# High parts of a seven-product pair in one tile of the large pool: a fp32 decoder block on one core of Trainium2

## The chip, the cores and the metric

One core of a Trainium2 chip runs the whole program. The metric is the device time of one execution in microseconds (us), taken as the median of several runs.

## The reference

One layer of a decoder on 256 tokens with a width of 2048, all in fp32. What matters here are its matrix products with large weights:

```python
u = rmsnorm(h, g_mix[i]);  proj = u @ w_in[i]
out_a = attn @ w_attn_br[i]          # sliding-window attention
out_s = y @ w_ssd_br[i]              # Mamba-2 SSD branch
merged = sigmoid(g_a) * out_a + sigmoid(g_s) * out_s
h = h + merged @ w_o[i]
f = rmsnorm(h, g_ffn[i])
h = h + (silu(f @ w_gate[i]) * (f @ w_up[i])) @ w_down[i]
h = h + sigmoid(rmsnorm(h, g_ple[i]) @ w_ple_gate[i]) * (p[i] @ w_ple_proj[i])
return rmsnorm(h, g_final)
```

## The kernel before

A fp32 weight is split into a high part (a cast to fp32r on ScalarE, ACT) and a low part (weight minus high part, on VectorE, DVE). A product is then three matmuls on TensorE (PE): high times high, high times low, low times high. PE does little else than these.

`wide_block` (L281) multiplies the 256 tokens (two blocks of 128) with two column blocks of 512 and runs over the contraction in k-pairs of 2 x 128. It serves the last gate columns of `w_in` (GSO, two calls), `w_ssd_br` (two), `w_o` (two), eleven blocks of gate and up (`hidden`, called hidden 0 to 10 here), and `w_down`, which is cut into thirds that run after hidden 3, 7 and 10 (two calls each). For each k-pair there are two kinds of work:

- A *plain* pair: for each of the two column blocks a load of 512 KB into a buffer `wr` (SP's queue, L298), the cast `wh` of 1024 columns (L309), the subtraction `wl` (L311), and 24 matmuls (L249) in all.
- A *seven-product* pair (two block products in seven instead of eight, for the pairs in `forms`; 40 in the program): two loads, four additions of 512 columns on DVE into `tr` (L329), then casts (L337) and subtractions (L338) of three items: the whole first load (1024 columns), one half of the second load (512 columns), and `tr` (2048 columns, into `th` and `tl`), and 21 matmuls.

Buffers come from rotating pools: `wraw` has 4 (for `wr`), `whi` 4 (for `wh`), `wlo` 3 (for `wl`), each of 1024 columns (4 KB per partition), and `big` 17 of 8 KB, for `tr`, `th`, `tl`, the token matrices and more. A tile waits until the buffer that it gets is no longer read.

`pump` calls queued small work between the k-pairs: transposes of results on PE (L150) with their copies to SBUF (L137, L132 on ACT, L139, L133 on DVE), the token sums that the seven-product pairs multiply with (`fsc`, `fm`, `hforms`, `aforms`, L256 to L278), and sums of squares (`junk`, L1037).

The order of the instructions on each engine is not written by hand: a scheduler places them when the program is built, by when it takes operands and buffers to be ready. Each engine then runs its own list in that order. So a change of buffers moves instructions.

Of the kernel before, what the change touches and what calls it, by code (L numbers as in the profile page):

```python
# [12 lines left out]
F32R = mybir.dt.float32r  # L13
# [5 lines left out]
P = 128  # L19
# [4 lines left out]
NB = 512  # L24
# [37 lines left out]
def block_kernel(ctx: ExitStack, tc: tile.TileContext, x, x_t, p_t, positions, vecs, rows, g_final,  # L62
# [7 lines left out]
    whi_p = ctx.enter_context(tc.tile_pool(name="whi", bufs=4))  # L70
    wlo_p = ctx.enter_context(tc.tile_pool(name="wlo", bufs=3))
# [5 lines left out]
    def big(shape, dtype=F32, name="big"):  # L77
        return big_p.tile(shape, dtype, name=name, tag="big")
# [18 lines left out]
    def pump(n):  # L97
        for _ in range(n):
            for q in (side, heads):
                if q:  # L100
                    q.popleft()()
# [179 lines left out]
    def wide_block(halves, lhs, nk, forms, pumps=1):  # L281

        psum.reverse()
        np_, ns = nk // 2, len(forms)  # L290
        c11, c12, c21, c22 = sums = [
            Sums(acc_tile, 2 * (np_ - ns) + (ns if i < 3 else 0)) for i in range(4)]
        shared, done = None, 0
        parts = [None] * 4

        def load(q, kp, dst):
            w, col0 = halves[q]
            nc.sync.dma_start(out=dst, in_=w[2 * kp * P:2 * (kp + 1) * P, col0:col0 + NB].rearrange(  # L298
                "(k p) n -> p k n", p=P))

        for kp in range(np_):
            ev, od = lhs(2 * kp), lhs(2 * kp + 1)
            tok = [[[x[:, t * P:(t + 1) * P] for x in k] for k in (ev, od)] for t in range(NT)]
            if kp not in forms:
                for q in range(2):
                    wr = wraw_p.tile([P, 2, NB], F32, name="wr", tag="wr")
                    load(q, kp, wr)
                    wh = whi_p.tile([P, 2, NB], F32R, name="wh", tag="wh")
                    nc.scalar.copy(out=wh, in_=wr)  # L309
                    wl = wlo_p.tile([P, 2, NB], F32R, name="wl", tag="wl")  # L310
                    nc.vector.tensor_tensor(out=wl, in0=wr, in1=wh.bitcast(F32), op=ALU.subtract)  # L311
                    for k in range(2):
                        for t in range(NT):
                            sums[2 * t + q].add(tok[t][k], (wh[:, k], wl[:, k]))
                    pump(pumps)
                continue
            if shared is None:
                shared = [Sums(aux_tile, ns) for _ in range(4)]
            q1, q5, q6, q7 = shared
            a, g2, f3, s3 = [[forms[kp][:, i, 0], forms[kp][:, i, 1]] for i in range(4)]  # L320
            raw = [wraw_p.tile([P, 2, NB], F32, name="wr", tag="wr") for _ in range(2)]
            for q in range(2):
                load(q, kp, raw[q])
            tr = big([P, 4, NB], F32, name="tr")
            for o, x, y in ((tr[:, 0], raw[0][:, 0], raw[1][:, 0]),
                            (tr[:, 1], raw[1][:, 0], raw[1][:, 1]),
                            (tr[:, 2], tr[:, 1], raw[0][:, 0]),
                            (tr[:, 3], tr[:, 2], raw[0][:, 1])):
                nc.vector.tensor_tensor(out=o, in0=x, in1=y, op=ALU.add)  # L329
            split = []  # L330
            for x, xh, xl in (
                    (raw[0], whi_p.tile([P, 2, NB], F32R, name="wh", tag="wh"),
                     wlo_p.tile([P, 2, NB], F32R, name="wl", tag="wl")),
                    (raw[1][:, 1:2], whi_p.tile([P, 2, NB], F32R, name="wh", tag="wh")[:, 1:2],
                     wlo_p.tile([P, 2, NB], F32R, name="wl", tag="wl")[:, 1:2]),
                    (tr, big([P, 4, NB], F32R, name="th"), big([P, 4, NB], F32R, name="tl"))):
                nc.scalar.copy(out=xh, in_=x)  # L337
                nc.vector.tensor_tensor(out=xl, in0=x, in1=xh.bitcast(F32), op=ALU.subtract)  # L338
                split.extend((xh[:, i], xl[:, i]) for i in range(x.shape[1]))
            b11, b21, b22, t1, t3, t2, t4 = split  # L340
            q1.add(tok[0][0], b11)
            c11.add(tok[0][1], b21)
            c12.add(f3, b22)
            q6.add(g2, t2)
            q7.add(s3, t3)
            q5.add(a, t1)
            c21.add(tok[1][1], t4)
            pump(2 * pumps)
            done += 1
            if done == ns:  # L350
                mid = big([P, 4, NB], F32, name="mid")
                parts = [mid[:, i] for i in range(4)]
                nc.scalar.copy(out=parts[0], in_=q1.tile)
                for o, x, y, op in ((3, 0, q6, ALU.subtract), (2, 3, q7, ALU.add),
                                    (1, 3, q5, ALU.add), (3, 2, q5, ALU.add)):
                    nc.vector.tensor_tensor(out=parts[o], in0=parts[x], in1=y.tile, op=op)
        return [x.tile for x in sums], parts
# [649 lines left out]
    for jj in range(2):  # L1007
        sums, parts = wide_block(column_pair(w_in, GSO, jj), lhs_u, KD, uforms)
        for i in range(4):
            settle(i, sums, parts)  # L1010
            nc.scalar.activation(out=parts[i], in_=parts[i], func=AF.Sigmoid,
                                 scale=r1[:, i // 2:i // 2 + 1])
        gates.append(parts)
    mforms = form_tiles((5,), "mforms")
    for jj in range(2):
        sums, parts = wide_block(column_pair(w_ssd_br, 0, jj), lambda k: stat(yT, k), KD, yforms)
        for i in range(4):
            t, c = i // 2, cols(2 * jj + i % 2)
            settle(i, sums, parts)
            nc.vector.scalar_tensor_tensor(out=parts[i], in0=parts[i], scalar=r2[:, t:t + 1],  # L1020
                                           in1=gates[jj][i], op0=ALU.mult, op1=ALU.mult)
            nc.vector.tensor_tensor(out=merged[t][:, c], in0=merged[t][:, c], in1=parts[i],
                                    op=ALU.add)
        for q in range(2):
            queue_flip(merged, mergedT, 2 * jj + q, None, mforms)
# [19 lines left out]
    for jj in range(2):  # L1045
        add_to_h(jj, *wide_block(column_pair(w_o, 0, jj), lambda k: stat(mergedT, k), KD, mforms))
        for q in range(2):
            queue_flip(h, hT, 2 * jj + q, V_GFFN, hforms)
            side.append(lambda j=2 * jj + q: square_sum(j, ssq3))
# [135 lines left out]
    for c in range(KD // 4):  # L1185
# [3 lines left out]
        wh = whi_p.tile([P, 2, NB], F32R, name="wh", tag="wh")  # L1189
        nc.scalar.copy(out=wh, in_=wr)  # L1190
        wl = wlo_p.tile([P, 2, NB], F32R, name="wl", tag="wl")
# [73 lines left out]
```

## Time and profile before

| | |
|---|---|
| median of 3 runs | 1595.82 us (1594.87 to 1597.53) |
| the profiled execution | 1594.49 us, its span 1592.8 us |
| busy: PE, DVE, ACT | 99%, 75%, 53% of the span |
| chain of work that ended last | PE 92%, DVE 2%, DMA 2%, ACT 2%, issue 1% |
| mean granted clock of PE | 0.998 |

How to read it: the busy share of PE is modelled and says only that it hardly rests. The places where it does rest, and what ends each rest, are in the waits and in the timeline. A row of the timeline gives the start, the time, engine, line and operation, output and inputs, and in brackets the idle time before it with what ended it. Loads are issued on SP; the view of DMA gives the time from issue to landing.

### The profile page before, as it was taken

How to read it: one execution, taken by the hardware profiler on the slowest of the kernel's cores; microseconds unless marked ns; L12 is line 12 of the kernel's file. 1: busy time of each engine (PE TensorE's matmuls, PEld its weight loads, DVE VectorE, ACT ScalarE, POOL GpSimd, SP SyncE). 2: the span in 40 equal slices, each digit the busy share in tenths (PEclk: the TensorE clock that was granted, in tenths of full speed). 3: DMA queues.
4: the chain of work that ended last, by engine and by line, in shares of the span. 5: the costliest groups of instructions: out<-in, count | busy, mean ns of one | idle time of the engine just before them, and what ended most of it. 6: DMA issues, size and time to landing. Idle time of an engine off the chain costs nothing.

```text
span 1592.8 us, 19985 instructions
## 1 busy us (share of the span) xinstructions
PE 1574.0 (99%) x7298; PEld 1300.5 (82%) x7298; DVE 1201.3 (75%) x1507; ACT 844.2 (53%) x1073; POOL 132.1 (8%) x136
## 2 busy tenths in 40 slices
PE   9999999999999999999999999999999999999997
PEld 7988888888888888788788888788888878888886
DVE  8776766666666768788888788887878788788874
ACT  6654665555644554445655554455545444556653
POOL 1014224143210000000000000000000000000000
PEclk9999999999999999999999999999999999999999
DMA  8666435555646666655566655566665566655672
GB/s 270 177 198 185 136 105 158 158 161 157 178 157 183 210 199 213 209 195 189 173 199 195 198 188 197 185 210 193 193 196 177 194 203 199 220 189 185 200 228 87
DMA packets 152562, 296.63 MB, mean 186 GB/s; under 512 B 9536, under 2 KB 9664, under 8 KB 152080
## 3 DMA queue, kind: packets, MB, share of 16 engines
q1 hardware_dynamic: 151168, 290.76, 58.3%
q0 software_dynamic: 576, 3.47, 0.7%
q8 instruction: 57, 0.93, 0.2%
q10 hardware_dynamic: 720, 1.14, 0.2%
q14 instruction: 41, 0.34, 0.1%
HBM read 293.23 MB, written 2.10 MB: 185 GB/s over the span
## 4 chain that ended last, share of the span: by engine, by line
PE 92%; DVE 2%; DMA 2%; ACT 2%; issue 1%; POOL 0%; POOLq 0%; DVEq 0%; SPq 0%; ACTq 0%
PE aux L249 29%; PE acc L249 27%; PE acc L204 9%; PE acc L206 9%; PE acc L205 9%; PE aux L150 1%; DMA wr<-in_w_in_dram 1%; PE aux L754 1%; DMA wr<-in_w_gate_dram 1%; ACT th L337 1%; PE acc L150 1%; DVE tl L338 1%; PE aux L935 1%; PE aux L693 0%; ACT sc L899 0%
## 5 line engine op out<-in xcount | busy, mean ns | idle before, releaser
L309 ACT CAST wh<-wr 128x1024 fp32r<-128x1024 f32 x280 | 293.6, 1053 | 269.4 <-PE acc L249 97.2
L311 DVE TENSOR_TENSOR wl<-wr,wh 128x1024 fp32r<-128x1024 f32 x280 | 337.3, 1221 | 88.2 <-issue 35.8
L195 DVE TENSOR_TENSOR wl<-wr,wh 128x1024 fp32r<-128x1024 f32 (+1 forms) x172 | 227.6, 1330 | 119.6 <-PE acc L205 87.4
L193 ACT CAST wh<-wr 128x1024 fp32r<-128x1024 f32 (+1 forms) x172 | 173.7, 1013 | 167.9 <-PE acc L206 125.6
L249 PE MATMUL aux<-wh,flipT 128*128 128x512 f32 x736 | 237.8, 392 | 0.0
L249 PE MATMUL acc<-wh,flipT 128*128 128x512 f32 x640 | 208.4, 393 | 0.0
L204 PE MATMUL acc<-wh,uT 128*128 128x512 f32 (+1 forms) x512 | 200.3, 391 | 0.7 <-ACT cb L481 0.7
L206 PE MATMUL acc<-wh,uT 128*128 128x512 f32 (+1 forms) x512 | 194.2, 379 | 0.0
L205 PE MATMUL acc<-wl,uT 128*128 128x512 f32 (+1 forms) x512 | 193.9, 379 | 0.0
L249 PEld LDWEIGHTS aux<-wh,flipT 128*128 128x128 f32 x736 | 138.1, 188 | 28.3
L249 PE MATMUL aux<-wl,flipT 128*128 128x512 f32 x368 | 143.8, 391 | 0.6 <-DVE wl L311 0.6
L337 ACT CAST wh<-wr 128x1024 fp32r<-128x1024 f32 x80 | 66.8, 837 | 140.2 <-PE aux L249 62.4
L249 PEld LDWEIGHTS acc<-wh,flipT 128*128 128x128 f32 x640 | 120.2, 188 | 24.6 <-ACT wh L337 0.2
L249 PE MATMUL acc<-wl,flipT 128*128 128x512 f32 x320 | 124.6, 389 | 0.0
L338 DVE TENSOR_TENSOR tl<-tr,th 128x2048 fp32r<-128x2048 f32 x40 | 91.7, 2292 | 26.2 <-ACT th L337 26.1
L204 PEld LDWEIGHTS acc<-wh,uT 128*128 128x128 f32 x512 | 96.3, 188 | 18.1 <-issue 1.4
L205 PEld LDWEIGHTS acc<-wl,uT 128*128 128x128 f32 x512 | 96.4, 188 | 17.6 <-issue 1.0
L206 PEld LDWEIGHTS acc<-wh,uT 128*128 128x128 f32 x512 | 96.2, 188 | 17.8
L337 ACT CAST th<-tr 128x2048 fp32r<-128x2048 f32 x40 | 76.5, 1911 | 51.7 <-DVE tr L329 51.7
L249 PE MATMUL aux<-wh,actT 128*128 128x512 f32 x292 | 95.3, 393 | 0.0
L249 PE MATMUL acc<-wh,actT 128*128 128x512 f32 x292 | 93.6, 390 | 0.0
L338 DVE TENSOR_TENSOR wl<-wr,wh 128x1024 fp32r<-128x1024 f32 x80 | 76.2, 954 | 7.8 <-PE aux L249 4.0
(476 smaller groups left out, 2741.4 us busy)
## 6 DMA issues: line engine op xcount, KB each, us to landing
wr<-in_w_in_dram SPq DMA_DIRECT2D x144, 512.0 KB, 3.7
wr<-in_w_gate_dram SPq DMA_DIRECT2D x88, 512.0 KB, 3.7
wr<-in_w_up_dram SPq DMA_DIRECT2D x88, 512.0 KB, 4.1
wr<-in_w_down_dram SPq DMA_DIRECT2D x88, 512.0 KB, 4.4
wr<-in_w_ssd_br_dram SPq DMA_DIRECT2D x32, 512.0 KB, 4.3
wr<-in_w_o_dram SPq DMA_DIRECT2D x32, 512.0 KB, 4.0
wr<-in_w_ple_gate_dram SPq DMA_DIRECT2D x32, 512.0 KB, 4.9
wr<-in_w_in_dram SPq DMA_DIRECT2D x32, 256.0 KB, 3.9
```

Of the source, the lines that this page charges most:

```text
L150: nc.tensor.transpose(out=ps[:, j, t * P:(t + 1) * P], in_=src[t][:, c:c + P], identity=ident)
L193: nc.scalar.copy(out=wh, in_=wr)
L195: nc.vector.tensor_tensor(out=wl, in0=wr, in1=wh.bitcast(F32), op=ALU.subtract)
L204: nc.tensor.matmul(o, hi[:, ts], wh[:, kk, cs], start=(k == 0), stop=False)
L205: nc.tensor.matmul(o, hi[:, ts], wl[:, kk, cs], start=False, stop=False)
L206: nc.tensor.matmul(o, lo[:, ts], wh[:, kk, cs], start=False, stop=(k == nk - 1))
L249: nc.tensor.matmul(self.tile, a, b, start=self.first, stop=self.left == 0)
L309: nc.scalar.copy(out=wh, in_=wr)
L311: nc.vector.tensor_tensor(out=wl, in0=wr, in1=wh.bitcast(F32), op=ALU.subtract)
L337: nc.scalar.copy(out=xh, in_=x)
L338: nc.vector.tensor_tensor(out=xl, in0=x, in1=xh.bitcast(F32), op=ALU.subtract)
L754: nc.tensor.matmul(ps[:, es], m[:, t, e, :], xd[:, t, 0, es], start=True, stop=True)
```

## The change

The pair takes one more buffer of the `big` pool, called `sh`, of four times 512 columns. It holds the high parts of the first load (2), of the half of the second (1), and the low part of that half (1). So a pair takes no buffer of `whi` (before: two) and one of `wlo` (before: two). The instructions are the same in number, kind and size.

```diff
             split = []
+
+            sh = big([P, 4, NB], F32R, name="sh")
             for x, xh, xl in (
-                    (raw[0], whi_p.tile([P, 2, NB], F32R, name="wh", tag="wh"),
-                     wlo_p.tile([P, 2, NB], F32R, name="wl", tag="wl")),
-                    (raw[1][:, 1:2], whi_p.tile([P, 2, NB], F32R, name="wh", tag="wh")[:, 1:2],
-                     wlo_p.tile([P, 2, NB], F32R, name="wl", tag="wl")[:, 1:2]),
+                    (raw[0], sh[:, 0:2], wlo_p.tile([P, 2, NB], F32R, name="wl", tag="wl")),
+                    (raw[1][:, 1:2], sh[:, 2:3], sh[:, 3:4]),
                     (tr, big([P, 4, NB], F32R, name="th"), big([P, 4, NB], F32R, name="tl"))):
                 nc.scalar.copy(out=xh, in_=x)
                 nc.vector.tensor_tensor(out=xl, in0=x, in1=xh.bitcast(F32), op=ALU.subtract)
```

The scheduler's order changes with it. On DVE, in the second block of `w_ssd_br`, with its seven-product pair, before:

```order
L329 TENSOR_TENSOR tr<-wr 128x512 x2
L311 TENSOR_TENSOR wl<-wr,wh 128x1024
L329 TENSOR_TENSOR tr<-tr,wr 128x512 x2
L338 TENSOR_TENSOR wl<-wr,wh 128x1024
L338 TENSOR_TENSOR tl<-tr,th 128x2048
L338 TENSOR_TENSOR wl<-wr,wh 128x512
L311 TENSOR_TENSOR wl<-wr,wh 128x1024 x3
```

and after:

```order
L329 TENSOR_TENSOR tr<-tr,wr 128x512
L338 TENSOR_TENSOR sh<-wr,sh 128x512
L329 TENSOR_TENSOR tr<-tr,wr 128x512
L338 TENSOR_TENSOR wl<-wr,sh 128x1024
L338 TENSOR_TENSOR tl<-tr,th 128x2048
L311 TENSOR_TENSOR wl<-wr,wh 128x1024 x3
```

The subtraction of 512 columns stood behind the one of 2048 and now stands ahead of it, and ahead of that of 1024.

On ACT, around the first seven-product pair of hidden 0 (`flipT`: copies of transposed h; `fsc`, `hforms`: token sums; `junk`: sums of squares), before:

```order
L309 CAST wh<-wr 128x1024 x6
L337 CAST wh<-wr 128x1024
L137 ACTIVATE flipT<-acc,vec 128x256 x2
L337 CAST wh<-wr 128x512
L137 ACTIVATE flipT<-acc,vec 128x256 x2
L256 ACTIVATE fsc<-acc,vec 128x256 x2
L309 CAST wh<-wr 128x1024
L1037 ACTIVATE junk,ssq_5704<-h 128x512
L277 CAST hforms<-fm 128x4x128
L1037 ACTIVATE junk,ssq_5704<-h 128x512 x2
L137 ACTIVATE flipT<-acc,vec 128x256
```

and after:

```order
L137 ACTIVATE flipT<-acc,vec 128x256
L256 ACTIVATE fsc<-acc,vec 128x256 x2
L1037 ACTIVATE junk,ssq_5692<-h 128x512 x2
L277 CAST hforms<-fm 128x4x128
L1037 ACTIVATE junk,ssq_5692<-h 128x512 x2
L137 ACTIVATE flipT<-acc,vec 128x256
L337 CAST sh<-wr 128x1024
L137 ACTIVATE flipT<-acc,vec 128x256
L337 CAST sh<-wr 128x512
L337 CAST th<-tr 128x2048
```

The pair's casts of 1024 and 512 columns (L337) stood ahead of `fsc`, and now stand behind it, `junk` and a further `flipT`.

On ACT, around the seven-product pairs of hidden 2 (hidden 6 reads alike), before:

```order
L337 CAST wh<-wr 128x1024
L132 CAST actT<-acc 128x512
L337 CAST wh<-wr 128x512
L132 CAST actT<-acc 128x512
L256 ACTIVATE fsc<-acc 128x256 x2
L309 CAST wh<-wr 128x1024
L277 CAST aforms<-fm 128x4x128
L309 CAST wh<-wr 128x1024
L337 CAST th<-tr 128x2048
```

and after:

```order
L132 CAST actT<-acc 128x512
L309 CAST wh<-wr 128x1024
L132 CAST actT<-acc 128x512
L309 CAST wh<-wr 128x1024
L256 ACTIVATE fsc<-acc 128x256 x2
L277 CAST aforms<-fm 128x4x128
L337 CAST sh<-wr 128x1024
L337 CAST sh<-wr 128x512
L337 CAST th<-tr 128x2048
L309 CAST wh<-wr 128x1024 x2
L337 CAST sh<-wr 128x1024
L337 CAST sh<-wr 128x512
```

The pair's casts moved behind two plain casts (L309), `fsc` and `aforms`.

## Rows read from the trace of the kernel before

**Rows 1.** The page's first part: busy time, share of the span, instructions.

```profile
PE 1574.0 (99%) x7298; PEld 1300.5 (82%) x7298; DVE 1201.3 (75%) x1507; ACT 844.2 (53%) x1073; POOL 132.1 (8%) x136
```

**Rows 2.** The chain that ended last: start, us, what.

```profile
583.92 27.20 PE aux L249 x120
```

**Rows 3.** Waits of PE: engine, line, waited for: total us, times, longest.

```profile
PE acc L249 <- DVE wl L338: 3.6, 3, 1.6
...
PE acc L249 <- DVE tl L338: 0.7, 1, 0.7
...
PE aux L249 <- DVE wl L311: 0.6, 1, 0.6
```

**Rows 4.** Lines 337, 338 and 329: ns min/median/max, first and last start, forms.

```profile
L337 ACT CAST wh<-wr x80: 610/838/1058, 507.4 to 1467.1; 128x1024 fp32r<-128x1024 f32 x40, 128x512 fp32r<-128x512 f32 x40
L337 ACT CAST th<-tr x40: 1895/1912/1919, 511.2 to 1468.2; 128x2048 fp32r<-128x2048 f32 x40
...
L338 DVE TENSOR_TENSOR wl<-wr,wh x80: 682/956/1226, 511.1 to 1472.4; 128x1024 fp32r<-128x1024 f32 x40, 128x512 fp32r<-128x512 f32 x40
...
L338 DVE TENSOR_TENSOR tl<-tr,th x40: 2286/2293/2294, 513.2 to 1470.2; 128x2048 fp32r<-128x2048 f32 x40
...
L329 DVE TENSOR_TENSOR tr<-wr x80: 680/686/694, 507.4 to 1464.4; 128x512 f32<-128x512 f32 x80
```

**Rows 5.** Timeline of PE, second GSO block and hidden 1: start, us, what.

```profile
532.86 0.50 PE L249 MATMUL aux<-wl,uforms 128*128 128x512 f32 x1 [0.15 <-DVE wl L338]
...
823.63 0.50 PE L249 MATMUL aux<-tl,hforms 128*128 128x512 f32 x1
```

**Rows 6.** Timeline of DVE and of PE, second block of w_ssd_br.

```profile
656.20 2.29 DVE L338 TENSOR_TENSOR tl<-tr,th 128x2048 fp32r<-128x2048 f32 x1 [0.85 <-ACT th L337]
...
659.15 0.50 PE L249 MATMUL acc<-wl,yforms 128*128 128x512 f32 x1 [1.65 <-DVE wl L338]
```

**Rows 7.** Timeline of ACT, PE and SP's queue, hidden 0.

```profile
765.78 1.05 ACT L337 CAST wh<-wr 128x1024 fp32r<-128x1024 f32 x1 [1.67 <-PE aux L249]
...
769.01 0.62 ACT L337 CAST wh<-wr 128x512 fp32r<-128x512 f32 x1 [0.78 <-PE aux L249]
...
775.62 0.46 ACT L137 ACTIVATE flipT<-acc,vec 128x256 fp32r<-128x256 f32 x1
...
775.05 0.48 PE L249 MATMUL acc<-wh,flipT 128*128 128x512 f32 x1
...
776.41 0.37 SPq L298 DMA_DIRECT2D wr<-in_w_gate_dram  x1
```

**Rows 8.** Hidden 2: ACT, SP's queue with the load's time to landing, PE.

```profile
859.71 0.66 ACT L256 ACTIVATE fsc<-acc 128x256 f32<-128x256 f32 x2 [0.76 <-DVE actT L133]
...
856.07 0.37 SPq L298 DMA_DIRECT2D wr<-in_w_up_dram  x1
...
wr<-in_w_up_dram SPq DMA_DIRECT2D x1, 512.0 KB, 4.1
...
863.50 0.39 PE L249 MATMUL acc<-wh,flipT 128*128 128x512 f32 x1
```

**Rows 9.** Hidden 4: SP's queue with the load's time to landing, PE.

```profile
1030.23 0.37 SPq L298 DMA_DIRECT2D wr<-in_w_up_dram  x1
...
wr<-in_w_up_dram SPq DMA_DIRECT2D x1, 512.0 KB, 5.5
...
1039.75 0.50 PE L249 MATMUL acc<-tl,hforms 128*128 128x512 f32 x1
```

**Rows 10.** Second w_o block: SP's queue, the first load's time to landing, PE.

```profile
740.35 7.46 SPq L298 DMA_DIRECT2D wr<-in_w_o_dram  x3
...
wr<-in_w_o_dram SPq DMA_DIRECT2D x1, 512.0 KB, 5.2
...
749.49 0.39 PE L249 MATMUL aux<-tl,mforms 128*128 128x512 f32 x1
```

**Rows 11.** Stretches: us, busy us by engine, granted clock, DMA share, GB/s.

```profile
657.00:659.20 2.20, 0.55 (x4) 0.13 (x2) 2.20 (x3) 2.20 (x4) 0.00 (x0) 1.00 0.58 194
```

## The prediction

> **What bounds the kernel now.** I read the page first, then the waits of TensorE (PE), the rows by line, and PE's timeline at every place where PE stood. PE is busy for 99% of the span [rows 1], and in an undisturbed stretch 120 matmuls of 512 columns follow each other in 27.20 us, 0.2267 us each [rows 2]. The change alters no matmul, cast, subtraction or load in number or size, so it can move the time only through the waits of PE. In the wide blocks PE waits for the vector engine (DVE) in few places, nearly all for low parts of seven-product pairs [rows 3]. Counting every start-to-start gap beyond 0.2267 us in those blocks, I find eighteen places that sum to 9.6 us. That is the ceiling of a gain. There is no such ceiling on a loss.
>
> **What one pair costs on its engines.** The casts of line 337 take 1.06 us (1024 columns), 0.61 (512) and 1.91 (the four sums), the subtractions of line 338 1.22, 0.69 and 2.29, and each of the four additions of line 329 0.69 [rows 4]. Consecutive instructions of one engine overlap by about 0.1 us. None of these changes. What changes is which buffer an instruction must wait for, and therefore the order that the scheduler writes down, shown in the section on the change: the 512 subtraction moves ahead of the 2048 one, both plain casts of a pair come in a bunch, and casts of the next plain k-pair move ahead of the 2048 cast. ScalarE (ACT) and DVE run their lists in that order, so a late operand at the head holds up all behind it.
>
> **Gains.** The order shortens the wait for the 512 low part, which now comes before the 2048 one.
> - Second GSO block: PE waited for a 512 low part at 532.86 [rows 5]; the gap is 0.42 us, and I take all of it.
> - Second w_ssd_br block: the 2048 subtraction ran from 656.20 to 658.49 and the 512 one behind it, and PE stood 1.65 us until 659.15 [rows 6], a gap of 1.92 with its after-effect. With the 512 one first, the 2048 one ends about 0.6 us later, 659.1, and PE wants it at 658.0, four matmuls after the last one ahead of the wait: a wait of 1.1 takes the place of 1.9. Gain 0.8 (0 to 1.9).
> - In six gate/up blocks (1, 3, 5, 7, 9, 10) PE waits a little for the 2048 low part, as at 823.63, where the matmul shows 0.50 [rows 5]; with the next one the gaps there come to 0.22. The changed order puts several matmuls of the plain pair ahead of it; this goes. 6 x 0.22 = 1.3.
>
> Sum of the gains: 2.5 us.
>
> **Losses.** Each is worked out as the time at which an operand is ready in the changed order, against the time at which PE gets there.
> - *First gate/up block (hidden 0).* Before, the 1024 cast of the pair ran at 765.78 and the 512 one at 769.01, long before PE used them at 775.05 [rows 7]. In the changed order both stand behind the transposes' copies, the row sums (junk) and the first copy (L137) of the last transpose, which ran at 775.62 [rows 7]. So the 1024 cast runs from 776.3 or 777.3 to 777.3 or 778.4, where PE wants it at 775.3: a wait of 2.0 to 3.1 us, I take 2.5. Its subtraction, a copy's, two additions, and the 512 one then stand ahead of the plain pair's subtraction, which ends at 781.9 to 783 where PE wants it about 1.2 us earlier. The next loads suffer too: the four raw buffers stay held until these subtractions are done, so the next load starts at about 780 where it started at 776.41 [rows 7], and the second pair of the block meets its low parts later, by 0.2 to 2 us, I take 1.2. Before, this block had gaps of 1.2 us that are replaced. Sum: 2.5 + 1.2 + 1.2 + 0.3 for the 512 part - 1.2 = +4.0 (2.0 to 6.5).
> - *Gate/up blocks 2 and 6.* The casts of the pair now stand behind a plain cast whose data were loaded from 856.07 on in 4.1 us [rows 8], thus at 860.2 and not sooner. That cast ends at 861.2; two copies, 0.66 together [rows 8], four small sums on DVE (to about 862.8) and a cast of 0.6 follow, then the 1024 cast, which ends at 864.5. PE wants it at 863.50 [rows 8]. The wait is 1.0. Behind it DVE does the pair's subtractions and two plain ones in a row without a pause, from 865.3 on, and ends the 2048 low part at 872.3. It stands 27 matmuls behind the pair's first, so in the old time PE would have got there at 863.50 + 27 x 0.2267 = 869.6: +2.7, and the loads behind it start 3 us later, so the next pair just makes it; +3.0 with 0.3 for that (1.5 to 4). Two blocks, +6.0.
> - *First gate/up block after w_down, twice (blocks 4 and 8).* The 2048 cast now stands behind the second plain cast, whose load started at 1030.23 and took 5.5 us [rows 9], landing at 1035.7. So cast to 1036.8, 2048 cast to 1038.6, low part to 1040.9. PE uses it in the new order five matmuls earlier than at 1039.75 [rows 9], 1038.6: +2.2, less 0.4 for the gap before it that is replaced. But the 512 waits of the two w_down blocks ahead (1.3 us and 2.05 us) go, and with them the loads start 0.7 or more sooner. Net +1.2 and +1.1 (0 to 2 each).
> - *Second w_o block.* The 2048 cast stands behind a plain cast whose load started at 740.35 and took 5.2 us [rows 10], 745.6. Cast to 746.7, 2048 cast to 748.6, low part to 750.9, wanted at 749.49 [rows 10]: +1.3 (0 to 2).
> - *First w_down blocks of the first two thirds:* the same with a smaller lateness, +0.1 each.
>
> In the other seventeen pairs the 2048 low part is at least 1.2 us ahead of its use before, which covers the 0.6 us that the 512 subtraction now puts ahead of it, so they cost nothing. Were a load late there too, each would cost up to 2 us as in w_o; that is in the rival "worse".
>
> **Sum.** -2.5 + 4.0 + 6.0 + 2.3 + 1.3 + 0.2 = +11.3 us. The profiled execution took 1594.49, so 1605.8; the median of the runs is 1.33 above that execution, so 1607.1, given as 1607.0. That is 0.7% slower.
>
> The waits now reach 2 to 3 us, so PE's clock matters. In the stretch 657.00 to 659.20, where PE was busy for 0.55 of 2.20 us, the granted clock was 1.00 [rows 11], the level of 2.4 GHz, and after the wait matmuls were back at their spacing at once. The Trainium skill, page "TensorE: Matmul & The Clock Gate", section "HAM oscillation — how this bites in real kernels", says that long enough idle gaps let the engine fall back to half the clock. The row shows it not to happen at 1.65 us of wait; no run here shows it at 3. The sum goes by the row; what the other would cost is a rival.
>
> **Rivals.**
> - *Faster.* The seven-product pairs no longer share the small pools, all the waits of [rows 3] go and nothing takes their place: up to -9.6 us, 1586 to 1592. Its place is the head of ACT's list at hidden 0, 2 and 6: it decides that way if the bunched casts find their data and ACT idle before 774 and 862. The 53% of ACT [rows 1] speaks for it; against it, that the list puts them behind work whose times [rows 7, 8] are set by PE's own transposes and by a load. Chance 0.06. The Trainium skill, page "Perfetto Trace Analysis", section "Optimization Strategy", reads a gap that returns as a sign that buffers ran out, which would favour this rival.
> - *No change that can be told.* The new waits just repay the old, because loads land sooner than before everywhere that I let them land as before: 1592.6 to 1599. A measurement of this kernel can tell about 0.2%, 3.2 us, from no change. Chance 0.07.
> - *Half the loss.* Only the pairs at hidden 0, 2 and 6 lose, at the low bounds: 2.0 + 3.0 - 2.5 and a little of the rest, 1598 to 1603. Chance 0.20, a quarter of it within 0.2%.
> - *Worse.* Raw buffers held longer make loads late in pairs that I hold to be covered, one after the other: 4 more pairs at 2 us, 1613 to 1620. Chance 0.09.
> - *The clock falls.* If three or four waits of 2 to 3 us each cost a stretch at 1.2 GHz, where a matmul needs twice 0.2267, a stretch of ten of them costs 2.3 us: with four, 9 more, 1616. Chance 0.03.
> - *The change does not do what it says.* The 8 KB tile could wait for one of the 17 buffers. In the changed order the cast into it waits for its load alone at the places I looked at, so I give this no chance of its own; it would look like the rival "worse".
>
> **How the numbers follow.** The forecast itself, 1603 to 1613, has 0.55. Low end 1597.2: the low bounds of all losses (2.0 + 3.0) less gains of 3.6 give +1.4 on the median; high end 1614.5: the high bounds (6.5 + 8 + 4 + 2) less gains of 1.7 give +18.8. What lies below it is the faster rival and half of "no change", above it most of "worse" and the clock. Faster by over 0.2%: 0.06. Within: 0.07 + 0.05 = 0.12. Slower: 0.55 + 0.15 + 0.09 + 0.03 = 0.82.
>
> **What would show it.** Right, if after the change PE waits at the first use of the 1024 cast in hidden 0 for 2 to 3 us on ACT (line 337) and about 1 us in gate/up blocks 2 and 6; if PE's waits on the 512 subtraction (now into the shared tile) are below 1 us in all; if the waits on the 2048 low part rise from 0.7 us to 6 or more; and if the load after the pair of hidden 0 is issued 3 to 4 us later than its PE work. Wrong, if ACT does those casts ahead of the use, if PE's total waits in the wide blocks stay under 9.6 us, or if the granted clock falls below 1.00 in the middle of the span.

## The result, and the profile after

The changed kernel takes 1614.32 us (median of 4 runs, 1611.2 to 1617.17), before 1596.18 (4 runs). The ratio is 1.0113 with a 95% interval of 1.0092 to 1.0134: 18 us slower, 1.1%. The profiled execution took 1611.2 us, span 1609.5, 16.7 longer than before's.

The page of the changed kernel, first and fourth part, answers to [rows 1]:

```profile
span 1609.5 us, 19889 instructions
PE 1579.7 (98%) x7298; PEld 1301.3 (81%) x7298; DVE 1198.6 (74%) x1507; ACT 847.3 (53%) x1073; POOL 134.2 (8%) x136
...
PE 85%; DVE 5%; DMA 5%; ACT 3%; issue 1%; POOL 0%; SPq 0%; POOLq 0%; DVEq 0%; ACTq 0%
```

The counts are as before, and the busy times of DVE and ACT differ by less than 0.4%. The chain that ended last has lost 7 points of PE to DVE, DMA and ACT: the work is the same, and PE waits more. Its waits, against [rows 3]:

```profile
PE acc L249 <- DVE tl L338: 4.0, 4, 1.8
PE acc L249 <- ACT sh L337: 3.3, 3, 2.1
PE acc L249 <- DVE wl L311: 2.2, 3, 1.3
PE aux L249 <- DVE tl L338: 2.0, 3, 0.8
PE acc L249 <- ACT th L337: 1.8, 2, 1.1
...
PE acc L249 <- DVE wl L338: 1.5, 2, 0.8
```

The wait that the change takes away is gone: the 3.6 us on the 512 low part were line 338 into `wl`, and no wait of a matmul on the subtraction into `sh` is listed (the weight loads wait 0.4 us for it in all; the 1.5 us left under `wl` are for the 1024 low part). In its place stand waits on casts (`sh`, `th`), on which no matmul waited before, on the 2048 low part (6.0 us where it was 0.9), and on plain low parts.

To see where, I summed every start-to-start gap of 512-column matmuls beyond 0.227 us by wide block, and took the difference to before. One execution of each kernel stands behind it. In blocks whose code was the same, such sums differed by up to 1.3 us between executions, so a single entry is good to about 1 us. The forecast's column holds its terms, with the 0.1 for each w_down block put to the gate/up block behind it.

| place | forecast, us | changed kernel, us |
|---|---|---|
| GSO | -0.4 | -0.4 |
| second w_ssd_br | -0.8 | +0.4 |
| second w_o | +1.3 | +1.1 |
| gate/up 0 | +4.0 | +3.9 |
| gate/up 2 and 6 | +6.0 | +2.9 + 3.1 |
| gate/up 1, 3, 5, 7, 9, 10 | -1.3 | -1.3 |
| w_down, first third, with gate/up 4 | +1.3 | +0.7 + 2.5 |
| w_down, second third, with gate/up 8 | +1.2 | -0.9 + 3.9 |

The entries sum to 15.9 us, of the 16.7 by which the span grew. Another 0.5 us were lost ahead of the first wide block, where the code is the same. No other wide block lost more than 0.1 us.

**Gate/up block 0.** ACT, SP's queue and PE around its first seven-product pair, against [rows 7]:

```profile
774.17 0.84 ACT L256 ACTIVATE fsc<-acc,vec 128x256 f32<-128x256 f32 x2 [0.55 <-DVE flipT L139]
...
776.13 0.61 ACT L277 CAST hforms<-fm 128x512 fp32r<-128x512 f32 x1
...
777.87 0.46 ACT L137 ACTIVATE flipT<-acc,vec 128x256 fp32r<-128x256 f32 x1
778.23 1.03 ACT L337 CAST sh<-wr 128x1024 fp32r<-128x1024 f32 x1
...
779.53 0.61 ACT L337 CAST sh<-wr 128x512 fp32r<-128x512 f32 x1
...
782.20 0.37 SPq L298 DMA_DIRECT2D wr<-in_w_gate_dram  x1
```

```profile
776.76 0.48 PE L249 MATMUL aux<-wh,flipT 128*128 128x512 f32 x1
779.32 0.66 PE L249 MATMUL acc<-sh,flipT 128*128 128x512 f32 x1 [2.08 <-ACT sh L337]
779.77 0.63 PE L249 MATMUL aux<-sh,flipT 128*128 128x512 f32 x1
...
782.08 0.63 PE L249 MATMUL aux<-sh,flipT 128*128 128x512 f32 x1
```

The 1024 cast stands behind the copies, the row sums, the token forms and the first copy of the last transpose, ends at 779.26, and PE stands for 2.08 us. The next load starts at 782.20, when the subtraction of the 512 part ends (781.49 plus 0.69). Then comes something that was forecast only as a small rival: the matmuls behind the wait start 0.43 us apart, not 0.23, and take 0.63 instead of 0.39. The stretches show what goes with it (columns: length, busy time by engine, granted clock, DMA share, GB/s):

```profile
776.60:779.30 2.70, 0.64 (x5) 0.32 (x3) 2.23 (x4) 2.70 (x8) 0.00 (x0) 1.00 0.00 0
779.30:783.00 3.70, 3.69 (x9) 2.55 (x10) 3.70 (x7) 1.03 (x3) 0.00 (x0) 0.54 0.00 0
783.00:787.00 4.00, 3.81 (x17) 2.83 (x16) 4.00 (x4) 2.59 (x2) 2.93 (x1) 1.00 0.92 291
1047.00:1053.00 6.00, 3.52 (x14) 2.55 (x14) 4.56 (x3) 3.92 (x4) 0.00 (x0) 1.00 0.61 200
...
1315.40:1318.90 3.50, 3.50 (x9) 2.79 (x10) 2.19 (x2) 1.07 (x2) 0.00 (x0) 0.52 0.34 78
```

After PE's wait the granted clock is 0.54 on average over 3.7 us, near the 1.2 GHz level, and 1.00 again afterwards. It is 0.52 from 1315.40 on, behind the waits of gate/up block 8. These are the only two falls in the wide blocks, and before there was none. Eight or nine matmuls 0.2 us late each make about 1.7 us per fall, so some 3.4 of the 16.7 us are the clock, which comes on top of the waits.

**Gate/up block 2.** The sum agrees with the forecast (+2.9, forecast +3.0), but not its parts. PE waits for the 1024 cast and then for its low part:

```profile
869.74 0.50 PE L249 MATMUL acc<-sh,flipT 128*128 128x512 f32 x1 [0.52 <-ACT sh L337]
871.68 0.50 PE L249 MATMUL acc<-wl,flipT 128*128 128x512 f32 x1 [0.74 <-DVE wl L338]
```

Behind these come 0.17 us for a plain low part and 0.21 us in the second pair. On the 2048 low part of the first pair, for which 2.7 us were worked out, PE does not wait. Block 6 reads alike (0.67, 0.75, 0.17 and 0.19).

**After w_down.** PE in gate/up block 8, against the low part of block 4 in [rows 9]:

```profile
1313.04 0.50 PE L249 MATMUL acc<-th,hforms 128*128 128x512 f32 x1 [1.12 <-ACT th L337]
1315.37 0.80 PE L249 MATMUL acc<-tl,hforms 128*128 128x512 f32 x1 [1.82 <-DVE tl L338]
1315.96 1.05 PE L249 MATMUL acc<-th,hforms 128*128 128x512 f32 x2
1316.82 0.63 PE L249 MATMUL acc<-tl,hforms 128*128 128x512 f32 x1
```

PE waits for the 2048 cast, does one matmul, and waits again for the subtraction that follows the cast; and then it runs at half the clock.

### The profile page after: what moved, and what is told of

Same layout as the page of the kernel before. It is cut to its first block, busy times and chain, and to the rows that moved or that the text cites. A ratio compares the mean times of both kernels' runs of the same rounds, so it can differ in the third digit from the quotient of the medians.

```text
span 1609.5 us, 19889 instructions
## 1 busy us (share of the span) xinstructions
PE 1579.7 (98%) x7298; PEld 1301.3 (81%) x7298; DVE 1198.6 (74%) x1507; ACT 847.3 (53%) x1073; POOL 134.2 (8%) x136
## 4 chain that ended last, share of the span: by engine, by line
PE 85%; DVE 5%; DMA 5%; ACT 3%; issue 1%; POOL 0%; SPq 0%; POOLq 0%; DVEq 0%; ACTq 0%
PE aux L249 26%; PE acc L249 24%; PE acc L204 9%; PE acc L206 9%; PE acc L205 9%; DVE wl L311 2%; DMA wr<-in_w_up_dram 2%; DMA wr<-in_w_down_dram 2%; DVE tl L338 1%; DVE tr L329 1%; DMA wr<-in_w_ssd_br_dram 1%; ACT th L337 1%; PE aux L150 1%; PE aux L754 1%; ACT wh L309 1%
## 5 line engine op out<-in xcount | busy, mean ns | idle before, releaser
L309 ACT CAST wh<-wr 128x1024 fp32r<-128x1024 f32 x280 | 294.9, 1054 | 360.7 <-PE aux L249 109.4
L311 DVE TENSOR_TENSOR wl<-wr,wh 128x1024 fp32r<-128x1024 f32 x280 | 336.6, 1221 | 61.9 <-PE aux L249 26.4
L249 PE MATMUL aux<-wh,flipT 128*128 128x512 f32 x688 | 220.6, 392 | 0.0
L249 PE MATMUL acc<-wh,flipT 128*128 128x512 f32 x592 | 189.6, 393 | 0.0
L249 PEld LDWEIGHTS aux<-wh,flipT 128*128 128x128 f32 x688 | 129.2, 188 | 26.6
L249 PEld LDWEIGHTS acc<-wh,flipT 128*128 128x128 f32 x592 | 111.1, 188 | 22.8
L329 DVE TENSOR_TENSOR tr<-wr 128x512 f32<-128x512 f32 x80 | 52.8, 688 | 69.9 <-DMA wr<-in_w_up_dram 29.5
L337 ACT CAST sh<-wr 128x1024 fp32r<-128x1024 f32 x80 | 65.9, 836 | 58.0 <-DMA wr<-in_w_up_dram 25.7
L337 ACT CAST th<-tr 128x2048 fp32r<-128x2048 f32 x40 | 76.5, 1912 | 33.7 <-DVE tr L329 33.7
L249 PE MATMUL aux<-wh,actT 128*128 128x512 f32 x272 | 87.5, 393 | 0.0
L249 PE MATMUL acc<-wh,actT 128*128 128x512 f32 x272 | 85.7, 390 | 0.0
```

The lines of the kernel that those rows point to most:

```text
L249: nc.tensor.matmul(self.tile, a, b, start=self.first, stop=self.left == 0)
```

## The experiments

Each run is compared with runs of the kernel before on the same chip, which took 1594.88 to 1596.32 us by chip. A run and the changed kernel are therefore compared by these ratios, and not by their times. Losses by block are the sums of gaps of the table, one execution each. The theory: what costs is the place of the casts in ACT's order at gate/up blocks 0, 2 and 6, and late loads at the head of that order elsewhere.

### Where the loss lies: e1 and e2

A flag chooses the form of a pair by block (e1: shared tile only in blocks 0, 2, 6; e2: everywhere else):

```diff
-            sh = big([P, 4, NB], F32R, name="sh")
+            if shared_tile:
+                sh = big([P, 4, NB], F32R, name="sh")
...
+            else:
+                plain = tuple(
+                    (x, whi_p.tile([P, 2, NB], F32R, name="wh", tag="wh")[:, s],
+                     wlo_p.tile([P, 2, NB], F32R, name="wl", tag="wl")[:, s])
+                    for x, s in ((raw[0], slice(0, 2)), (raw[1][:, 1:2], slice(1, 2))))
```

> The shared tile only in the six seven-product pairs of gate/up blocks 0, 2 and 6; the other 34 pairs as before. Theory (place in ACT's list: there the casts into the shared tile stand behind the token sums and come too late): the losses read at these blocks in the changed kernel, 4.1 + 3.0 + 3.2 us, stay, so 10 us slower than before, about 1606; PE waits on the 1024 cast about 2.3 + 0.7 + 0.8 us. Rival (every changed pair costs the same, since raw buffers are held longer): 6 of 40 pairs, 2.7 us, about 1599.

> The complement: the shared tile in all pairs but those of gate/up blocks 0, 2 and 6. Theory: the rest of the loss, 18.1 - 10.3 = 7 to 8 us slower than before, about 1603.5, with no wait of PE on a 1024 cast and no stretch below full granted clock at 780 us. Rival (every pair costs the same): 34 of 40, 15 us, about 1611.

e1: 1605.7 us against 1596.32, ratio 1.0051 (1.0034 to 1.0067), +9.4. e2: 1602.66, 1.004 (1.0027 to 1.0053), +6.3. Six of forty pairs carry about half of the loss, as the theory has it; by the rival (each pair the same) it would be 2.7 us. The two parts sum to 15.7 of the 18.1. The clock is in both: each of the two executions had two falls of it (blocks 0 and 6; blocks 4 and 8).

### Which part of the tile: e3 and e5

```diff
-                     wlo_p.tile([P, 2, NB], F32R, name="wl", tag="wl")[:, 1:2]),
+                     sl[:, 0:1]),
```

is e3 against the kernel before (`sl` is a tile of the large pool), and e5 against the changed kernel:

```diff
-                    (raw[1][:, 1:2], sh[:, 2:3], sh[:, 3:4]),
+                    (raw[1][:, 1:2], sh[:, 2:3], wlo_p.tile([P, 2, NB], F32R, name="wl", tag="wl")[:, 1:2]),
```

> Only the low part of the 512 item in a tile of the large pool; the high parts stay in the small pool as before. Theory: the casts stay where they were, so the losses at gate/up blocks 0, 2 and 6 are absent and the waits on the 512 low part (3.6 us before) go, while the 2048 low part comes 0.6 us later: between 4 us faster and 4 us slower than before, 1592 to 1600. Rival (the order of DVE, 512 ahead of 2048, is what costs): most of the 18 us stays, 1608 to 1614.

> Only the high parts in a tile of the large pool; the low part of the 512 item stays in the small one as before. Theory (the casts' place on ACT is the cause at gate/up blocks 0, 2 and 6, and the low part has nothing to do with it): the losses there stay, 3.9 + 2.9 + 3.1 us, so at least 1606, with PE waiting there on the 1024 cast. Rival (the tile that holds high and low parts, so that subtractions and matmuls share it, is the cause): as before, 1594 to 1599.

e3: 1595.42 us, 0.9994 (0.9985 to 1.0004): no difference that can be told. The gains of the 512 part are in it (w_down -0.7 and -1.7), with a loss of 1.1 in block 4 against them. e5: 1617.35, 1.0139 (1.0125 to 1.0152), no faster than the change, with PE waiting for the cast into `sh` for 4.5 us. So moving the low part alone costs nothing in the sum, and putting the high parts into the large pool is what costs.

### ACT's order behind the pair: e4

```diff
+                    if last_th:
+                        tc.add_manual_dep(plain.ins, last_th[-1].name, mybir.DependencyInfo(
+                            mybir.DependencyClass.NoSync, mybir.DependencyReason.DATA))
```

> The changed kernel, with one order edge per pair: the casts of the plain pairs that follow stand behind the 2048 cast on ACT. Theory: the waits on the 2048 cast and its low part after w_down and in w_o (0.8 + 2.1, 1.3 + 2.1 and 0.9 us in the changed kernel) shrink to 2 us in all, the losses at blocks 0, 2 and 6 stay, so 5 us faster than the changed kernel, about 1609. Rival (late loads, not the order, hold the 2048 part): as the changed kernel, 1614, or slower since the plain casts now wait too.

1612.8 us, 1.0104 (1.0089 to 1.0119): as the changed kernel. The loss in w_o went (0.0 where it was 1.1), and others took its place: block 0 +6.1 for +3.9, the two thirds of w_down +2.2 for +0.7 and +0.9 for -0.9. Its waits show how:

```profile
PE aux L249 <- DVE tl L343: 5.5, 5, 1.8
PE acc L249 <- DVE tl L343: 3.9, 5, 0.9
PE acc L249 <- ACT th L342: 3.0, 3, 1.8
PE aux L249 <- ACT wh L311: 2.2, 5, 0.5
```

Plain casts (`wh`) now make PE wait. My expectation fell, and the rival came: the order of these casts alone does not hold the 2048 part. In block 4 the 2048 cast starts 11.9 us after the block's first matmul, as in the changed kernel (11.8), although no plain cast stands ahead of it. The first load of the pair now starts 1.3 us after that matmul, where it started 4.7 us ahead of it.

### Late loads: e6 and e7

```diff
-    wraw_p = ctx.enter_context(tc.tile_pool(name="wraw", bufs=4))
-    whi_p = ctx.enter_context(tc.tile_pool(name="whi", bufs=4))
+    wraw_p = ctx.enter_context(tc.tile_pool(name="wraw", bufs=5))
+    whi_p = ctx.enter_context(tc.tile_pool(name="whi", bufs=3))
```

e6 is this on the changed kernel, e7 on e2.

> The changed kernel with 5 instead of 4 buffers for raw weights and 3 instead of 4 for high parts of plain pairs (same space). Theory: at gate/up blocks 0, 2 and 6 the cast stands behind token sums whatever the loads do, so about 10 us of loss stay there; in the other places (second w_ssd_br, second w_o, second w_down, blocks 4 and 8) it is the late load that holds up a cast at the head of ACT's list, so with loads started one buffer earlier their 8 us go: about 1606. Rival (all of it is ACT's order): as the changed kernel, 1614. Rival (all of it is late loads): as before or faster, 1596.

> The same 5 and 3 buffers, with the shared tile in all pairs but those of gate/up blocks 0, 2 and 6. Theory: both causes are away, what is left are the gains: 1592 to 1597, no wait of PE above 1 us in the wide blocks. Rival (all of it is ACT's order): 1602 as without the fifth buffer.

e6: 1602.85 us, 1.0048 (1.0034 to 1.0062), by ratio about 10 us less than the changed kernel. The first two thirds of w_down with blocks 4 and 8 went from +6.2 to -4.1 us, w_o's second block to 0.0; blocks 0, 2 and 6 kept 3.1 + 1.3 + 1.4. New waits came in the first w_o block (+1.4). At block 4 the order around the 2048 cast is that of the changed kernel, with both plain casts ahead of it, and only the loads are earlier. Counted from the block's first matmul, the second plain load starts at 2.8 us where it started at 6.1, and the 2048 cast at 7.6 where it started at 11.8. Block 8 reads alike. So late loads are the cause at blocks 4 and 8. In w_down and w_o the order moved too, and e4 had removed w_o's loss by order alone, so there the two are not separated. In two places the theory failed. The second w_ssd_br block did not gain (+1.3, where the changed kernel has +0.4). And blocks 0, 2 and 6 did not keep their 10 us whatever the loads do, but 5.8.

The buffers have a price as well. Ahead of the first wide block e6, e7 and e10, the three runs with five and three, lost 2.2 to 3.1 us against the kernel before (all other runs at most 0.8), with PE waiting 1.8 us for low parts of line 195.

e7: 1601.78, 1.004 (1.0026 to 1.0054): the expectation of 1592 to 1597 was wrong. The first w_o block lost 2.2 us and block 0 lost 4.5. In block 0 PE waits 0.57 and 0.81 us for plain casts and 0.61 for a plain low part, and then the clock falls; 6.8 us at half of it make 3.4 of the 4.5 (columns as above):

```profile
786.40:793.00 6.60, 6.11 (x14) 4.79 (x15) 5.73 (x6) 1.85 (x2) 0.00 (x0) 0.50 0.92 299
```

There the pair in its old form takes two of only three buffers for high parts, and the plain cast stands behind the row sums and token forms on ACT. That the buffers put it there is likely, but no run tested it by itself (e10, whose pair takes none, lost 0.2 there).

### Why the casts stand late in blocks 0, 2 and 6: e9 and e10

In the kernel before, the 1024 cast of the first pair in blocks 0, 2 and 6 ran 10.9, 7.1 and 7.1 us ahead of the first addition into `tr`, a tile of the large pool. In the changed kernel it runs 0.6 to 0.9 us behind that addition. On ACT it stands at block 0 right behind the first copy into a transposed token matrix, at blocks 2 and 6 behind the cast into the token forms, also tiles of that pool. e9 uses the tile earlier in the program:

```diff
+        if first_touch:
+            early = big([P, 4, NB], F32R, name="sh")
+            nc.gpsimd.memset(early.bitcast(F32)[:, 3, 0:1], 0.0)
...
+                                 hforms, first_touch=j in (0, 2, 6))
```

> The changed kernel, with one element of the shared tile of the first pair in gate/up blocks 0, 2 and 6 set to zero by GpSimd at the head of the block, so that the program uses the tile before it uses the token forms and the copies of the transposes. Theory (the scheduler hands out buffers of a pool in the program's order of first use, so the casts into the tile could not be placed ahead of the writers of those other tiles of the same pool): the casts go back ahead of the token sums, the waits on the 1024 cast (3.3 us) vanish, and 10 us of loss with them: about 1604, as with the old form in these blocks (1602.7). Rival (the tile is late for lack of one of the 17 buffers, or the blocks are slow for another reason): as the changed kernel, 1614.

> Both remedies: the early use of the tile, and 5 buffers for raw weights with 3 for high parts. Theory: the 5.8 us that the run with 5 raw buffers still lost in gate/up blocks 0, 2 and 6 go: 1602.9 - 5.8 = 1597, about as before. Rival (with 3 buffers for high parts the plain casts wait for a buffer instead, as they did in block 0 with the old form, 4.5 us): 1602.

e9: 1602.94 us, 1.0051 (1.0035 to 1.0068), by ratio about 10 us less than the changed kernel and within 2 us of e2. ACT in block 0 of e9:

```profile
764.72 1.05 ACT L341 CAST sh<-wr 128x1024 fp32r<-128x1024 f32 x1 [1.53 <-DMA wr<-in_w_gate_dram]
...
767.60 0.62 ACT L341 CAST sh<-wr 128x512 fp32r<-128x512 f32 x1 [0.88 <-DMA wr<-in_w_up_dram]
768.12 0.47 ACT L137 ACTIVATE flipT<-acc,vec 128x256 fp32r<-128x256 f32 x1
...
780.88 0.61 ACT L277 CAST hforms<-fm 128x512 fp32r<-128x512 f32 x1
```

Both casts are back ahead of the token forms, as soon as their loads land, and no wait on them is left. Blocks 0, 2 and 6 lose 0.9 + 0.5 + 0.5. In these blocks it was neither a lack of a buffer, since e9 holds one for longer, nor the tile itself. It was the place of the tile's first use in the program: the order fits a scheduler that places the first write of a tile behind the first writes of other tiles of its pool that the program uses earlier. That rule is read from these orders, not from the scheduler. e10: 1597.26, 1.0013 (1.0004 to 1.0023): with both remedies 2.4 of the 18 us are left, about what the five and three buffers cost ahead of the first wide block. The 5.6 us from e6 to e10 agree with the 5.8 that e6 still lost in blocks 0, 2 and 6.

### The step that was mis-sized: e11 and e12

With e1's flag, the shared tile only in blocks 4 and 8 (e11), and only in the first two thirds of w_down (e12).

> The shared tile only in gate/up blocks 4 and 8, the first after w_down. Theory (their own order does it: the 2048 cast stands behind the second plain cast of the next pair, whose load lands late): these blocks lose 2.5 to 4 us each as in the changed kernel, the rest as before: 1595.5 + 6 = 1601. Rival (the loss there comes from the w_down blocks ahead, whose changed order delays the loads): 0 to 1 us each, 1596.

> The complement for that place: the shared tile only in the w_down blocks of the first two thirds. Theory: the 512 waits of w_down go (1.0 and 1.9 us) and blocks 4 and 8 lose nothing, 1592.5. Rival (these blocks move the loads and casts of blocks 4 and 8 as well): losses of 2.5 us and more at blocks 4 and 8, 1598 or more.

e11: 1598.47 us against 1595.7, 1.0012 (1.0002 to 1.0022). e12: 1597.11, 1.0006 (0.9994 to 1.0018). At blocks 4 and 8 e11 loses 1.2 and 0.7 us, e12 1.7 and 0.9, and the changed kernel 2.5 and 3.9, of which 1.7 at block 8 are the clock. Neither theory nor rival came: each form alone costs part of it, though with entries good to about 1 us the parts are not sharp. In e12 only the second third of w_down gains (-2.3); the first loses 0.7, as in the changed kernel. The load of the second plain cast in block 4, in the changed kernel (block from 1034.1) and in e12 (from 1025.3), against [rows 9] (from 1025.0):

```profile
1040.18 0.37 SPq L298 DMA_DIRECT2D wr<-in_w_up_dram  x1
...
1031.44 0.37 SPq L298 DMA_DIRECT2D wr<-in_w_up_dram  x1
```

It starts 6.1 us after the block's first matmul in both, where it started at 5.2 before, and in e11, whose w_down blocks have the old form, it starts at 5.2. So the changed w_down blocks delay the next block's loads by 0.9 us.

### A version that beats both: e8

The shared tile only in GSO and gate/up blocks 1, 3, 5, 7, 9, 10, e3's form in the first two thirds of w_down, the old form elsewhere:

```diff
+        sums, parts = wide_block(column_pair(w_in, GSO, jj), lhs_u, KD, uforms, form='shared')
...
+                                 hforms, form='shared' if j in (1, 3, 5, 7, 9, 10) else 'before')
...
+                                     form='before' if last else 'low'))
```

> The shared tile only where it took a wait away without making one (GSO, gate/up blocks 1, 3, 5, 7, 9, 10), only the low part in the large pool in the first two thirds of w_down, the rest as before. Theory: gains of 0.4 + 1.3 + 0.7 + 1.7 us add up to 4.1 less up to 1 in gate/up block 4: 1592 to 1594 where before has 1596.3. Rival (each gain is given back at the next block, where loads then bind): 1596, no difference.

1591.25 us against 1595.5, 0.9973 (0.9963 to 0.9982): 4.3 us faster, where 4.1 less up to 1 were expected. By block GSO, w_down and five of the six gate/up blocks gained (block 1 did not), and block 4 lost 0.7. Of the waits on low parts in the wide blocks, 3.0 us are left:

```profile
PE aux L249 <- DVE wl L311: 1.7, 3, 0.7
...
PE acc L249 <- DVE wl L350: 1.1, 1, 1.1
...
PE acc L249 <- DVE tl L350: 0.2, 1, 0.2
```

## Why the prediction was right, and where it was off

The direction and the mechanism were right: slower, 0.82 forecast, because casts of ACT come late where the scheduler put them behind other work. The size was too small. The measured 1614.32 lies just inside the range (to 1614.5, which its own terms make 1614.6), 7.3 above the forecast and outside the 1603 to 1613 that had 0.55. Of the 7.3 us, 4.6 are terms of the wide blocks, 0.8 lie outside them, and 1.8 come from the median, which is 3.1 above the profiled execution and was taken as 1.33; that execution was the fastest of the four.

Of the signs named, these came: PE waits 2.08 us for the 1024 cast in block 0 (2 to 3 forecast), no matmul waits on the 512 subtraction, the load behind the first pair of block 0 starts 4.1 us later counted from the block's start (3 to 4 forecast), and the waits on the 2048 low part rise to 6.0 us. The last came in other places than worked out: 3.6 of the 6.0 are at blocks 4 and 8, and 0.4 at blocks 2 and 6, where 5.4 were forecast. The waits on the 1024 cast in blocks 2 and 6 are 0.5 and 0.7 us (about 1 forecast). One sign of being wrong came too: the granted clock fell below 1.00 in the middle of the span.

- *Gains* of GSO and of the six gate/up blocks: as forecast to 0.2 us.
- *Second w_ssd_br block*, "Gain 0.8 (0 to 1.9)": wrong, +0.4. The 512 wait went and the 2048 wait came, as said (0.79 us at 660.46, forecast 1.1). But PE also waits for a plain low part, whose subtraction stands behind two additions, as before, and the additions wait for a load (rows of PE and DVE in the changed kernel):

```profile
654.38 0.50 PE L249 MATMUL acc<-wl,yT 128*128 128x512 f32 x1 [0.52 <-DVE wl L311]
660.46 0.50 PE L249 MATMUL aux<-tl,yforms 128*128 128x512 f32 x1 [0.79 <-DVE tl L338]
651.89 1.29 DVE L329 TENSOR_TENSOR tr<-wr 128x512 f32<-128x512 f32 x2 [2.69 <-DMA wr<-in_w_ssd_br_dram]
```

  That load is late because the weight loads ahead of it, issued from 635 on, land about 2 us later than before and free their buffers later. Before, the two transfers of 1 MB that bring x into `h`, tiles of the large pool, started 17 us apart. In the changed kernel the first starts 17 us later, and both run beside these loads. The transfers and the time to landing of the load at 635, before and after:

```profile
616.18 0.60 POOL L1030 DMA_DIRECT2D h<-in_x_dram  x1 [152.56 <-PE aux L249]
633.17 0.54 POOL L1030 DMA_DIRECT2D h<-in_x_dram  x1 [16.38 <-DVE mid L1020]
wr<-in_w_ssd_br_dram SPq DMA_DIRECT2D x1, 512.0 KB, 7.7
...
633.28 0.60 POOL L1030 DMA_DIRECT2D h<-in_x_dram  x1 [169.14 <-PE aux L150]
634.46 0.54 POOL L1030 DMA_DIRECT2D h<-in_x_dram  x1 [0.57 <-DVE merged L1022]
wr<-in_w_ssd_br_dram SPq DMA_DIRECT2D x1, 512.0 KB, 9.5
```

  The first transfer is that late in every run whose w_ssd_br pairs take one more buffer of the large pool (e3 among them), and early in the others (e1, e8, e11, e12). So here the 17 buffers are most likely short, for `h` and not for the shared tile, which alone the last rival looked at; no run with more buffers tested it. The term looked only at the pair's own low parts.
- *Blocks 0, 2 and 6*, +10.0: measured +9.9, and e1 gives +9.4 by time. That the sums agree is in part luck. Block 0 has 1.7 us of clock, which was not in the sum; without them it would be near the low bound of 2.0. The wait on the 1024 cast came as worked out, but the plain low part, for which 1.2 us were counted, made PE wait 0.19, and the second pair cost less than the 1.2 counted. In blocks 2 and 6 the wait on the 2048 low part did not come, and waits on the cast and on its own low part made up for it.
- *Second w_o block*, +1.3: +1.1.
- *Blocks 4 and 8*, "Net +1.2 and +1.1": this step failed in size, +3.2 and +3.0 with w_down. The late 2048 part was there as worked out (PE waits 0.65 and 1.12 us for the cast, and 1.82 for its low part in both blocks). The credit was not: I let the loads start 0.7 us sooner because the waits of w_down go, and they start 0.9 us later (e12). In the first third PE waits instead at 1021.07 for a plain low part, behind three additions and the 512 subtraction on DVE, the first of which had waited for its load until 1017.26:

```profile
1021.07 0.50 PE L249 MATMUL acc<-wl,actT 128*128 128x512 f32 x1 [1.31 <-DVE wl L311]
```

  In the second third the waits went (-0.9), and 1.7 of block 8's 3.9 us are the clock. e6 shows that earlier loads remove the loss of both blocks.
- *The clock rival*, 0.03: it came, beside the forecast rather than in its place, with two falls and 3.4 us where it was given four and 9. The sum went by a row at 1.65 us of wait and put the clock at nothing.
- *"Worse"*, loads late one after the other in covered pairs: no. No block beyond those named lost more than 0.1 us.
- *"Faster"* by the Trainium skill's reading of a gap that returns ("Perfetto Trace Analysis", "Optimization Strategy"): the returning gap on the 512 low part did go when its buffer came from the larger pool (e3, e8). Whether buffers had run out there or the order on DVE made the gap is not shown, since the order changed with the buffer. The kernel as a whole did not become faster, because the casts' order changed too. e8 has the gain without that.

## What to carry to other kernels

Where a scheduler orders the engines at build time, moving a tile to another pool can move instructions even where no buffer is short, as in gate/up block 0: look at what the same pool's tiles are written by just ahead of the new tile's first write, in the order of the program. Compare the changed order at the stage borders, where casts are wanted early and other work of the pool is late, and change only the places that gain. Look as well at who takes the pool's buffers next: here the transfers of x came 17 us later and crowded the weight loads. When a wait is removed, follow what comes next on the same engine: here a plain subtraction took over, and in the next block a later load.

## What the runs showed of the hardware

The granted clock fell to the lower level, 0.50 to 0.54 of full, behind waits of PE and came back while PE was busy. In the changed kernel it fell after one wait of 2.08 us (block 0) and after waits of 1.12 and 1.82 us with a matmul between (block 8). After waits of 0.65 and 1.82 us in block 4 it stayed at 1.00, and the 1.65 us before the change did not lower it [rows 11]. Shorter waits lowered it in other runs: 1.39 us, with two of 0.16 and 0.15 behind it, in block 0 of e6. Alike waits did not act alike: in e9 it stayed at 1.00 after 0.87 and 1.83 us (block 4) and fell after 0.96 and 1.83 (block 8), and in e2 it fell in block 4 after 0.41 and 1.83, less than the changed kernel had there. So one execution without a fall, as the row at 1.65 us, does not show that such a wait is free. The Trainium skill ("TensorE: Matmul & The Clock Gate", "HAM oscillation — how this bites in real kernels") says that long idle gaps let the engine fall back to half the clock. The level agrees (0.50 to 0.54); here waits of 1.4 to 2.1 us were enough, at times.

Transfers that run together took longer: a weight load of 512 KB took 9.5 us beside two transfers of 1 MB, and 7.7 us beside one, at the same place of the second w_ssd_br block.
